# All sums of h's blocks and all lo splits on VectorE in a new order; the first gate and up pairs start with products of plain blocks

## The chip, the cores and the metric

The kernel runs on one core of a Trainium2 chip. The metric is the device time of one execution in microseconds, the median of several runs; smaller is better. The profile is of one execution, whose own time stands in the table below. Engines: TensorE (PE for matmuls, PEld for weight loads), VectorE (DVE), ScalarE (ACT), GpSimd (POOL), and SyncE (SP), whose queue issues most DMAs.

## The reference, cut to what matters

A trunk of two layers on x of 1024 tokens by 1024 channels, all float32. Layer 0 mixes tokens by sliding-window attention, layer 1 by a chunked gMLP gating unit (SGU); a conv-gated FFN follows each. The change concerns the input projections `h @ w_in` of the two FFNs and of the SGU, where h is the normalised x.

```python
def chunked_sgu(h, w_in, ln_g, ln_b, w_s, b_s, w_out):   # w_in: 1024 x 6144
    z = jax.nn.gelu(h @ w_in)
    u, v = jnp.split(z, 2, axis=-1)
    v = layer_norm(v, ln_g, ln_b)
...
    return (u * sv.reshape(B, S, SGU_HALF)) @ w_out

def conv_gated_ffn(h, w_in, conv_w, conv_b, w_out):       # w_in: 1024 x 5632
    g, u = jnp.split(h @ w_in, 2, axis=-1)
    gp = jnp.pad(g, ((0, 0), (CONV_WIDTH - 1, 0), (0, 0)))
    g = conv_b + sum(conv_w[k] * gp[:, k:k + S] for k in range(CONV_WIDTH))
    return (jax.nn.gelu(g) * u) @ w_out
...
    x = x + rms_norm(h, norm_mix_post[i])
    h = conv_gated_ffn(rms_norm(x, norm_ffn_pre[i]), ...)
    x = x + rms_norm(h, norm_ffn_post[i])
```

## The kernel before

**Split operands.** Every float32 operand of a matmul is kept as two tiles: hi, a cast to the narrower fp32r on ScalarE, and lo = operand - hi, a `tensor_tensor` subtraction. A product is three matmuls (hi·hi, hi·lo, lo·hi; `passes`). hi always comes from ScalarE. lo is made by VectorE, except that `split_eng` gives every third weight split to GpSimd; it serves `unit` (a whole weight column block, 128x1024), the `split` of `pair_unit` (128x512) and that of v's weights in `sgu` (128x1024).

**h.** `pre_norm` normalises a tile of 128 tokens; its deferred `transposes` turn it by TensorE into a PSUM bank, half a tile at a time, cast it to `hhi` and subtract to `hlo`. For the second half of tiles 0 to 3 the subtraction is done by GpSimd, which can't read PSUM, so ScalarE first copies the bank back to SBUF (L206).

**Strassen-Winograd pairs.** Two weight column blocks are multiplied with h as a 2x2 block product with seven products (`TERMS`) in place of eight: four combine sums of weight blocks S1 to S4 (`weight_sums`, made for each pair) with T1 to T3 or a plain block of h, and A22 meets T4. The sums T1 to T4 of h's blocks are made once per projection by `Blocks.steps`, in two halves q of 128x1024 each: T1 = h1a - h0a, T2 = h1b - T1, T3 = h1b - h1a, T4 = h0b - T2, with lo parts added, and each split into hi and lo (L560 the cast on ScalarE, L561 the subtraction). Before, T1 and T2 are summed on VectorE, T3 and T4 on GpSimd, and all are split on ScalarE and VectorE. `steps` is a generator that is advanced between the yields of the plain projections and then run to its end.

**The order of products.** `chain` gives it: A11·B11 into bank a, copied to p1; S2·T2 into b, u2 = b + p1; A12·B21 added on a, which is output (0,0); S1·T1 added on b, u4 = b + p1; S3·T3 into c, output (1,1) with u4; S4·B22 added on b, output (0,1); A22·T4 added on c, output (1,0) with u2. Every product of a pair is 12 matmuls of 512 columns (L683). In the SGU's v stage each block of weights uses the same seven products of 48 matmuls of 256 columns (L1138); its first block already begins with A11·B11, A12·B21 and S4·B22, on banks of their own.

**An FFN.** Columns 0 and 1 of g and u are projected plainly (`part`, `in_proj`, L140), first on the first half of the tokens, which are ready first, then on the second. Meanwhile T is made. Then ten gate pairs and ten up pairs alternate (`pair_unit`, `pair_chain`), with the convolution and the gelu between. `rawp` has two buffers, the two raw weight tiles of one pair; `wp` has eight, for the seven splits of a pair and one more. The result goes to DRAM and is read back by the out phase, which multiplies it with w_out.

**What sets the order.** The kernel runs in a TileContext that lays all instructions out before the launch: each engine has one queue, executed in order, and a planner fills these queues by a simulated timeline, in which, of the instructions that are ready, the one that stands first in the program goes first. So an engine's order can differ from the program's where something that stands later is ready sooner. Only part of the out phase fixes VectorE's order by hand. Weight loads go through SP's queue (L635 for the pairs).

## Time and profile before

| | |
|---|---|
| median of 3 runs (lowest, highest) | 2571.59 us (2565.28, 2573.16) |
| the profiled execution: time, span | 2569.5 us, 2567.8 us |
| TensorE matmuls busy | 2434.5 us, 95% of the span |
| TensorE weight loads busy | 2043.2 us, 80% |
| VectorE busy | 1848.3 us, 72% |
| ScalarE busy | 1047.4 us, 41% |
| GpSimd busy | 725.9 us, 28% |
| mean granted clock of TensorE | 0.982 of full speed |

Times in the rows are microseconds from the start of the span. Busy time is the time in which an engine executes; a share near 100% on TensorE means that matmuls follow each other without a gap, not that each is at its peak. The granted clock is a share of 2.4 GHz; 0.5 is the lower of its two levels. A duration includes the filling of the engine's pipeline, so instructions that follow each other start somewhat closer than their durations say.

### The profile page before, as it was taken

Reading aid. Unit: us, or ns where it says so; the run is one execution under the profiler, and the core shown is the slowest. Engines: PE = TensorE matmul, PEld = TensorE weight load, DVE = VectorE, ACT = ScalarE, POOL = GpSimd, SP = SyncE. Lnnn points to the kernel's source line nnn. Section 1 sums busy time; section 2 is a strip of 40 time slices with the busy share of each in tenths; the row PEclk is TensorE's granted clock in tenths of the full one; section 3 lists DMA queues with packets and bytes.
Section 4 is the critical chain, followed back from the end, with each engine's and each line's share of the span. In section 5 each row is a group of like instructions: output and inputs, shape, how many; then the busy total and the mean of one; then the engine's idle time right before and its main releaser. Section 6 shows DMA issues by size and latency. Waiting matters only on the chain.

```text
span 2567.8 us, 33884 instructions
## 1 busy us (share of the span) xinstructions
PE 2434.5 (95%) x12472; PEld 2043.2 (80%) x12472; DVE 1848.3 (72%) x2991; ACT 1047.4 (41%) x1941; POOL 725.9 (28%) x666
## 2 busy tenths in 40 slices
PE   7999988999999899979999999899997999998997
PEld 6877777888888687879997888688796888886886
DVE  5766699767666677796556765577898667666777
ACT  4655573333333444533332332444543333334443
POOL 3000035211112211361138887302254112112011
PEclk9999998999999999989999999999998999999999
DMA  7222141222226953423224445964221222249642
GB/s 221 67 49 55 50 149 49 75 90 90 67 91 212 249 151 77 156 75 116 91 90 148 141 136 184 299 203 93 90 95 48 88 90 78 80 133 286 178 98 99
DMA packets 267062, 310.50 MB, mean 121 GB/s; under 512 B 30126, under 2 KB 195344, under 8 KB 266896
## 3 DMA queue, kind: packets, MB, share of 16 engines
q1 hardware_dynamic: 249040, 275.82, 33.4%
q0 software_dynamic: 17856, 32.51, 7.5%
q8 instruction: 98, 1.61, 0.3%
q14 instruction: 68, 0.56, 0.1%
HBM read 220.72 MB, written 65.01 MB: 111 GB/s over the span
## 4 chain that ended last, share of the span: by engine, by line
PE 74%; DVE 11%; DMA 8%; issue 3%; POOL 2%; ACT 1%; SPq 1%; DVEq 0%; POOLq 0%; ACTq 0%
PE mm L683 25%; PE ob L683 10%; PE mm L772 9%; PE mm L140 6%; PE mm L1138 5%; PE ob L772 3%; PE tb L772 3%; PE ob L243 3%; DMA raw<-in_ffn_w_out 2%; PE ob L1138 2%; DVE osum L535 2%; DMA raw<-ad 2%; PE tb L1268 1%; DMA raw<-ads 1%; DVE tsum L535 1%
## 5 line engine op out<-in xcount | busy, mean ns | idle before, releaser
L683 PE MATMUL mm<-T,wsum 128*128 128x512 f32 x2496 | 601.2, 392 | 8.1 <-DVE T L535 2.9
L683 PEld LDWEIGHTS mm<-T,wsum 128*128 128x128 f32 x2496 | 467.5, 188 | 108.5 <-DVE T L535 3.9
L772 PE MATMUL mm<-osum 128*128 128x512 f32 x1644 | 400.4, 399 | 32.6 <-ACT acc L841 17.6
L772 PEld LDWEIGHTS mm<-osum 128*128 128x128 f32 x1644 | 312.5, 192 | 106.7 <-ACT acc L841 19.3
L535 DVE TENSOR_TENSOR osum<-raw,osum 128x512 fp32r<-128x512 f32 x372 | 246.1, 692 | 126.3 <-ACT osum L714 126.2
L714 ACT CAST osum<-raw 128x512 fp32r<-128x512 f32 x372 | 217.1, 619 | 284.0 <-PE tb L772 95.9
L683 PE MATMUL ob<-hhi,wsum 128*128 128x512 f32 x832 | 281.5, 397 | 22.4 <-DVE wsum L535 11.1
L642 ACT CAST wsum<-sums 128x512 fp32r<-128x512 f32 x208 | 127.5, 618 | 299.3 <-DVE sums L535 224.8
L683 PEld LDWEIGHTS ob<-hhi,wsum 128*128 128x128 f32 x832 | 158.2, 191 | 56.8 <-DVE wsum L535 11.6
L1253 POOL TENSOR_SCALAR vn<-vn,mv,rv 128x128 f32<-128x128 f32 x192 | 188.6, 994 | 45.0 <-DMA vn<-vd 21.2
L535 POOL TENSOR_TENSOR wsum<-sums,wsum 128x512 fp32r<-128x512 f32 x70 | 103.8, 1482 | 268.9 <-ACT wsum L642 227.7
L683 PE MATMUL ob<-hlo,wsum 128*128 128x512 f32 x416 | 164.6, 396 | 0.0
L535 DVE TENSOR_TENSOR wsum<-sums,wsum 128x512 fp32r<-128x512 f32 x138 | 103.4, 750 | 67.4 <-ACT wsum L642 66.6
L642 ACT CAST wsum<-raw 128x512 fp32r<-128x512 f32 x156 | 95.7, 619 | 132.7 <-PE mm L683 85.5
L772 PE MATMUL ob<-osum 128*128 128x512 f32 x480 | 131.7, 393 | 11.5 <-DVE osum L535 7.5
L683 PE MATMUL mm<-hhi,wsum 128*128 128x512 f32 x416 | 137.5, 391 | 1.6 <-DVE pu L538 1.6
L140 PE MATMUL mm<-hlo,whi 128*128 128x256 f32 (+1 forms) x416 | 136.6, 329 | 1.8 <-DVE hlo L208 1.8
L140 PE MATMUL mm<-hhi,whi 128*128 128x256 f32 (+1 forms) x416 | 136.6, 331 | 0.0
L140 PE MATMUL mm<-hhi,wlo 128*128 128x256 f32 (+1 forms) x416 | 135.9, 328 | 0.0
L997 DVE SCALAR_TENSOR_TENSOR cv<-gs,cw,cv 128x1024 f32<-128x1024 f32 (+1 forms) x96 | 124.3, 1299 | 12.4 <-ACT cv L995 11.9
L535 POOL TENSOR_TENSOR wsum<-raw,wsum 128x512 fp32r<-128x512 f32 x50 | 68.5, 1370 | 223.9 <-ACT wsum L642 179.6
L772 PE MATMUL tb<-osum 128*128 128x512 f32 x480 | 129.9, 389 | 0.0
(251 smaller groups left out, 4933.1 us busy)
## 6 DMA issues: line engine op xcount, KB each, us to landing
raw<-in_ffn_w_in SPq DMA_DIRECT2D x88, 512.0 KB, 3.9
ad<-cv SPq DMA_DIRECT2D x40, 512.0 KB, 3.8
raw<-ad SPq DMA_DIRECT2D x28, 512.0 KB, 6.4
raw<-in_ffn_w_out SPq DMA_DIRECT2D x28, 512.0 KB, 13.7
raw<-in_sgu_w_in SPq DMA_DIRECT2D x28, 512.0 KB, 4.0
xs<-xt SPq DMA_DIRECT2D x24, 512.0 KB, 3.2
vn<-vd SPq DMA_DIRECT2D x48, 256.0 KB, 3.8
ads<-ut SPq DMA_DIRECT2D x24, 512.0 KB, 5.0
```

Of the source, the lines that this page charges most:

```text
L140: nc.tensor.matmul(ps[:, cs], a[:, k, :], b[:, k, cs], start=n == 0, stop=n == 3 * KC - 1)
L243: nc.tensor.matmul(ps, a, b[:, half_of(nh)], start=n == 0 and not begun, stop=n == end, skip_group_check=begun)
L535: (eng or nc.vector).tensor_tensor(out=out, in0=a, in1=b, op=ALU.subtract)
L642: nc.scalar.copy(out=t[:, 0], in_=src)
L683: nc.tensor.matmul(bank, x, y, start=first and n == 0, stop=n == 3 * H4 - 1, skip_group_check=True)
L714: nc.scalar.copy(out=t[:, 0], in_=src)
L772: nc.tensor.matmul(self.banks[t], u, v, start=self.first and g == 0 and m == 0, stop=last and self.more is None and m == 2, skip_group_che ...
L997: nc.vector.scalar_tensor_tensor(out=cv, in0=gs[j][:, k + t0:k + t0 + n], scalar=tap_w(k, j), in1=cv, op0=ALU.mult, op1=ALU.add)
L1138: nc.tensor.matmul(bank[r][:, q * NQ:(q + 1) * NQ], x, y, start=first and q == 0 and m == 0, stop=m == 3 * H4 - 1, skip_group_check=True)
L1253: nc.gpsimd.tensor_scalar(out=vn[:, t, :], in0=vn[:, t, :], scalar1=mv[:, tt, 0:1], scalar2=rv[:, tt:tt + 1], op0=ALU.subtract, op1=ALU.mult)
L1268: nc.tensor.matmul(sv[:, t, :], vn[:, t, :], gws[(j + i) // 3][0], start=True, stop=True)
```

## The change

1. `split_eng` goes. Every weight split (`unit`, `pair_unit`, v's `split`) is done by VectorE.
2. In `transposes` the second half of tiles 0 to 3 is treated like all others: VectorE subtracts from the PSUM bank, and ScalarE's copy back to SBUF is gone.
3. `Blocks.steps` does all sums on VectorE. It makes T1 and T2 of both halves q first, splitting T2 and then T1, and only then T4 and T3 of each half. T4 is built in T2's temporary tile.
4. In an FFN the first gate pair and the first up pair use a new `first_chain` with the order A11·B11, A12·B21 (both on bank a), S4·B22 on a bank d of its own; then S2·T2 and S1·T1 on b; then S3·T3 and A22·T4 on c. `weight_sums` is called with `first`, which brings A12 and S4 forward. The gate's first five products are issued, then the up pair's weights and its first three products, then the rest of both. Later pairs are as before.
5. For the first column block of that pair the convolution, the multiplication and the output transfer are done in halves of 512 tokens, in tiles of `cvp`, which has four buffers in place of three.

```diff
--- before.py
+++ after.py
@@ -98,12 +98,6 @@
         nc.sync.dma_start(out=t, in_=row.partition_broadcast(P))
         return t
 
-    lo_turn = [0]
-
-    def split_eng():
-        lo_turn[0] += 1
-        return nc.gpsimd if lo_turn[0] % 3 == 0 else nc.vector
-
     def unit(src_aps, shape):
 
 
@@ -114,7 +108,7 @@
         hi = wp.tile(shape, F32R, name="whi", tag="w")
         lo = wp.tile(shape, F32R, name="wlo", tag="w")
         nc.scalar.copy(out=hi, in_=raw)
-        split_eng().tensor_tensor(out=lo, in0=raw, in1=hi.bitcast(F32), op=ALU.subtract)
+        nc.vector.tensor_tensor(out=lo, in0=raw, in1=hi.bitcast(F32), op=ALU.subtract)
         return hi, lo
 
     ALLS = (slice(None),)
@@ -198,14 +192,7 @@
                 for k in range(4):
                     nc.tensor.transpose(out=tp[:, k, :], in_=xn[:, tok(4 * q + k)], identity=ident)
                 nc.scalar.copy(out=hhi[:, ks], in_=tp)
-                eng = nc.vector
-                if q == 1 and t < 4:
-
-                    eng = nc.gpsimd
-                    back = xn[:, half_of(q)].rearrange("p (k q) -> p k q", q=P)
-                    nc.scalar.copy(out=back, in_=tp)
-                    tp = back
-                eng.tensor_tensor(out=hlo[:, ks], in0=tp, in1=hhi.bitcast(F32)[:, ks], op=ALU.subtract)
+                nc.vector.tensor_tensor(out=hlo[:, ks], in0=tp, in1=hhi.bitcast(F32)[:, ks], op=ALU.subtract)
 
         deferred.append(transposes)
 
@@ -563,33 +550,35 @@
             def temp():
                 return work.tile([P, 2, HALF], F32, name="tsum", tag="work")
 
-            for q in range(2):
-                ka, kb = slice(2 * q, 2 * q + 2), slice(H4 + 2 * q, H4 + 2 * q + 2)
-                t3 = temp()
-                sub_(t3, f(h1)[:, kb], f(h1)[:, ka], nc.gpsimd)
-                add_(t3, t3, f(l1)[:, kb], nc.gpsimd)
-                sub_(t3, t3, f(l1)[:, ka], nc.gpsimd)
-                yield
+            ks = [(slice(2 * q, 2 * q + 2), slice(H4 + 2 * q, H4 + 2 * q + 2)) for q in range(2)]
+            t2s = []
+            for q, (ka, kb) in enumerate(ks):
                 t1 = temp()
                 sub_(t1, f(h1)[:, ka], f(h0)[:, ka])
                 add_(t1, t1, f(l1)[:, ka])
                 yield
                 sub_(t1, t1, f(l0)[:, ka])
-                yield
                 t2 = temp()
                 sub_(t2, f(h1)[:, kb], t1)
                 yield
                 add_(t2, t2, f(l1)[:, kb])
                 split("T2", q, t2)
+                yield
                 split("T1", q, t1)
+                t2s.append(t2)
                 yield
+            for q, (ka, kb) in enumerate(ks):
+
+                sub_(t2s[q], f(h0)[:, kb], t2s[q])
+                add_(t2s[q], t2s[q], f(l0)[:, kb])
+                t3 = temp()
+                sub_(t3, f(h1)[:, kb], f(h1)[:, ka])
+                yield
+                add_(t3, t3, f(l1)[:, kb])
+                sub_(t3, t3, f(l1)[:, ka])
                 split("T3", q, t3)
                 yield
-                t4 = temp()
-                sub_(t4, f(h0)[:, kb], t2, nc.gpsimd)
-                yield
-                add_(t4, t4, f(l0)[:, kb], nc.gpsimd)
-                split("T4", q, t4)
+                split("T4", q, t2s[q])
                 yield
 
         def __getitem__(self, name):
@@ -627,7 +616,7 @@
         order = (0, 3, 1, 4, 5, 2, 6) if first else range(7)
         return [out[i] for i in order]
 
-    def pair_unit(w, c0, c1):
+    def pair_unit(w, c0, c1, first=False):
 
         raws = []
         for col in (c0, c1):
@@ -640,11 +629,11 @@
         def split(src):
             t = wp.tile([P, 2, H4, P], F32R, name="wsum", tag="w")
             nc.scalar.copy(out=t[:, 0], in_=src)
-            sub_(t[:, 1], src, t.bitcast(F32)[:, 0], split_eng())
+            sub_(t[:, 1], src, t.bitcast(F32)[:, 0])
             return t
 
         return weight_sums(raws[0][:, :H4], raws[0][:, H4:], raws[1][:, :H4], raws[1][:, H4:],
-                           sa[:, 0], sa[:, 1], sb[:, 0], sb[:, 1], split)
+                           sa[:, 0], sa[:, 1], sb[:, 0], sb[:, 1], split, first)
 
     def chain(products, p1, u2, u4, a, b, c, out):
 
@@ -672,23 +661,49 @@
         out(1, 0, c, u2)
         yield
 
+    def pair_product(wsum, name, blocks):
+        def go(bank, first):
+            n = 0
+            for k in range(H4):
+                for x, y in passes(wsum[:, 0, k, :], wsum[:, 1, k, :], *blocks[name](k)):
+                    nc.tensor.matmul(bank, x, y, start=first and n == 0, stop=n == 3 * H4 - 1,
+                                     skip_group_check=True)
+                    n += 1
+        return go
+
     def pair_chain(ws, blocks, out):
-
-
-        def product(wsum, name):
-            def go(bank, first):
-                n = 0
-                for k in range(H4):
-                    for x, y in passes(wsum[:, 0, k, :], wsum[:, 1, k, :], *blocks[name](k)):
-                        nc.tensor.matmul(bank, x, y, start=first and n == 0, stop=n == 3 * H4 - 1,
-                                         skip_group_check=True)
-                        n += 1
-            return go
 
         pu = gainp.tile([P, 2, HALF], F32, name="pu", tag="gpost")
         u2 = gainp.tile([P, 2, HALF], F32, name="u2", tag="gpre")[:, 0]
         a, b, c = out_bank(), mm_bank(), mm_bank()
-        yield from chain([product(w, t[1]) for w, t in zip(ws, TERMS)], pu[:, 0], u2, pu[:, 1], a, b, c, out)
+        yield from chain([pair_product(w, t[1], blocks) for w, t in zip(ws, TERMS)], pu[:, 0], u2, pu[:, 1], a, b, c,
+                         out)
+
+    def first_chain(ws, blocks, out, p1):
+
+        go = [pair_product(w, t[1], blocks) for w, t in zip(ws, TERMS)]
+        a, d = out_bank(), out_bank()
+        go[0](a, True)
+        nc.scalar.copy(out=p1, in_=a)
+        go[2](a, False)
+        out(0, 0, a, None)
+        go[5](d, True)
+        yield
+        u4 = gainp.tile([P, 2, HALF], F32, name="pu", tag="gpost")[:, 0]
+        u2 = gainp.tile([P, 2, HALF], F32, name="u2", tag="gpre")[:, 0]
+        b = mm_bank()
+        go[1](b, True)
+        add_(u2, b, p1)
+        go[3](b, False)
+        add_(u4, b, p1)
+        nc.scalar.copy(out=p1, in_=u4)
+        out(0, 1, d, p1)
+        yield
+        c = mm_bank()
+        go[4](c, True)
+        out(1, 1, c, u4)
+        go[6](c, False)
+        out(1, 0, c, u2)
 
 
     NPAIR = 6
@@ -998,7 +1013,7 @@
                                                in1=cv, op0=ALU.mult, op1=ALU.add)
             nc.scalar.activation(cv, cv, AF.Gelu_apprx_tanh, bias=tap_w(3, j))
 
-        with tc.tile_pool(name="gsp", bufs=2) as gsp, tc.tile_pool(name="cvp", bufs=3) as cvp:
+        with tc.tile_pool(name="gsp", bufs=2) as gsp, tc.tile_pool(name="cvp", bufs=4) as cvp:
 
             def part(j, half, parts):
                 if half == 0:
@@ -1008,7 +1023,7 @@
                 ps = in_proj(gu[j], h, half, parts)
                 yield
                 nc.scalar.copy(out=gs[j][:, 2 + half * HALF:2 + (half + 1) * HALF], in_=ps)
-                cv = cvp.tile([P, HALF], F32, name="cv")
+                cv = cvp.tile([P, HALF], F32, name="cv", tag="cv")
                 conv(j, cv, half * HALF, HALF)
                 ps = in_proj(uu[j], h, half, parts)
                 yield
@@ -1027,8 +1042,12 @@
                     run(part(j, half, 1), bs, bs, bs, bs, bs)
             run(bs)
 
-            for j in range(2 * PLAIN_FFN, nfc, 2):
+            def gate(j, first=False):
+
                 cv = {}
+
+                def cv_of(i, jj):
+                    return cv[i, jj] if first and i == 0 else cv[i][:, half_of(jj)]
 
                 def g_out(i, jj, ps, rest):
                     dst = gs[j + i][:, 2 + jj * HALF:2 + (jj + 1) * HALF]
@@ -1036,19 +1055,44 @@
                         nc.scalar.copy(out=dst, in_=ps)
                     else:
                         add_(dst, ps, rest)
-                    if i != jj:
+                    if first and i == 0:
+                        cv[i, jj] = cvp.tile([P, HALF], F32, name="cv", tag="cv")
+                        conv(j, cv[i, jj], jj * HALF, HALF)
+                    elif i != jj:
                         cv[i] = work.tile([P, S], F32, name="cv", tag="work")
                         conv(j + i, cv[i], 0, S)
 
                 def u_out(i, jj, ps, rest):
-                    dst = cv[i][:, half_of(jj)]
+                    dst = cv_of(i, jj)
                     if rest is not None:
                         add_(rest, ps, rest)
                         ps = rest
                     nc.vector.tensor_tensor(out=dst, in0=ps, in1=dst, op=ALU.mult)
-                    if i != jj:
+                    if first and i == 0:
+                        nc.sync.dma_start(out=ad[j][:, half_of(jj)], in_=dst)
+                    elif i != jj:
                         nc.sync.dma_start(out=ad[j + i], in_=cv[i])
 
+                return g_out, u_out
+
+            j0 = 2 * PLAIN_FFN
+            g_out, u_out = gate(j0, True)
+            gw = pair_unit(fw_in[layer], j0 * P, (j0 + 1) * P, True)
+            new_gs(j0)
+            new_gs(j0 + 1)
+            gc = first_chain(gw, blocks, g_out, cvp.tile([P, HALF], F32, name="p1", tag="cv"))
+            next(gc)
+            next(gc)
+            uw = pair_unit(fw_in[layer], DFF + j0 * P, DFF + (j0 + 1) * P, True)
+            uc = first_chain(uw, blocks, u_out, cvp.tile([P, HALF], F32, name="p1", tag="cv"))
+            next(uc)
+            for _ in gc:
+                pass
+            for _ in uc:
+                pass
+
+            for j in range(j0 + 2, nfc, 2):
+                g_out, u_out = gate(j)
                 gw = pair_unit(fw_in[layer], j * P, (j + 1) * P)
                 new_gs(j)
                 new_gs(j + 1)
@@ -1112,7 +1156,7 @@
                 hi = wp.tile([P, H4, NQ], F32R, name="vhi", tag="w")
                 lo = wp.tile([P, H4, NQ], F32R, name="vlo", tag="w")
                 nc.scalar.copy(out=hi, in_=src)
-                sub_(lo, src, hi.bitcast(F32), split_eng())
+                sub_(lo, src, hi.bitcast(F32))
                 return hi, lo
 
             for n in range(PLAIN_V, nb):
```

## Rows read from the trace of the kernel before

**Rows 1.** Stretches: busy us (instructions) of PE, PEld, DVE, ACT, POOL; clock; DMA.
```profile
330.00:372.00 42.00, 35.66 (x205) 26.49 (x204) 40.99 (x83) 30.06 (x75) 16.33 (x22) 1.00 0.36 127
...
400.00:460.00 60.00, 45.78 (x264) 39.76 (x264) 58.46 (x42) 21.15 (x31) 42.67 (x17) 0.89 0.12 39
460.00:805.00 345.00, 345.00 (x1524) 285.77 (x1523) 241.72 (x318) 125.66 (x188) 60.79 (x60) 1.00 0.29 91
...
1098.00:1144.00 46.00, 33.36 (x211) 30.94 (x209) 45.86 (x30) 15.32 (x19) 32.42 (x10) 0.90 0.24 79
...
1901.00:1963.00 62.00, 46.14 (x247) 38.54 (x247) 59.62 (x41) 21.00 (x31) 40.95 (x17) 0.83 0.14 42
```

**Rows 2.** Timeline, TensorE's matmuls: start, us, line, tiles, count, idle before.
```profile
419.75 0.40 PE L683 MATMUL ob<-hhi,wsum 128*128 128x512 f32 x1
...
814.78 0.50 PE L683 MATMUL mm<-hhi,wsum 128*128 128x512 f32 x1 [0.78 <-DVE pu L538]
...
820.40 0.84 PE L772 MATMUL mm<-osum 128*128 128x512 f32 x3
...
1107.23 0.40 PE L1138 MATMUL ob<-vhi,hhi 128*128 128x256 f32 x2
...
1918.83 0.40 PE L683 MATMUL ob<-hhi,wsum 128*128 128x512 f32 x1
...
2323.60 1.75 PE L772 MATMUL mm<-osum 128*128 128x512 f32 x7
```

**Rows 3.** Stretches, matmuls of L683 and of L1138 alone (count in brackets).
```profile
380.00:830.00 450.00, 385.61 (x1680) 0.98 0.30 94
...
1098.00:1180.00 82.00, 60.13 (x452) 0.92 0.28 91
```

**Rows 4.** Waits of TensorE, first FFN and SGU: us in total, times, longest.
```profile
PE ob L683 <- DVE wsum L535: 11.1, 1, 11.1
...
PE mm L1138 <- ACT T L560: 6.2, 1, 6.2
...
PE ob L1138 <- DVE vlo L535: 2.7, 1, 2.7
```

**Rows 5.** Timeline, VectorE.
```profile
399.94 2.92 DVE L535 TENSOR_TENSOR tsum<-hhi,hhi 128x1024 f32<-128x1024 f32 x1
402.90 3.32 DVE L538 TENSOR_TENSOR tsum<-tsum,hlo 128x1024 f32<-128x1024 f32 x1
...
412.44 0.68 DVE L535 TENSOR_TENSOR wsum<-sums,wsum 128x512 fp32r<-128x512 f32 x1
413.04 1.21 DVE L538 TENSOR_TENSOR tsum<-tsum,hlo 128x1024 f32<-128x1024 f32 x1
414.18 0.74 DVE L997 SCALAR_TENSOR_TENSOR cv<-gs,cw,cv 128x512 f32<-128x512 f32 x1
414.84 1.21 DVE L535 TENSOR_TENSOR T<-tsum,T 128x1024 fp32r<-128x1024 f32 x1
...
435.71 3.43 DVE L535 TENSOR_TENSOR wsum<-raw,wsum 128x512 fp32r<-128x512 f32 x2
...
458.57 0.69 DVE L538 TENSOR_TENSOR gs<-mm,pu 128x512 f32<-128x512 f32 x1
...
1155.25 1.21 DVE L535 TENSOR_TENSOR T<-tsum,T 128x1024 fp32r<-128x1024 f32 x1
```

**Rows 6.** Timeline, GpSimd.
```profile
401.86 3.27 POOL L538 TENSOR_TENSOR tsum<-tsum,hlo 128x1024 f32<-128x1024 f32 x1
```

**Rows 7.** Groups by line on GpSimd: count, busy us, mean ns, idle before.
```profile
L535 POOL TENSOR_TENSOR wsum<-sums,wsum 128x512 fp32r<-128x512 f32 x70 | 103.8, 1482 | 268.9 <-ACT wsum L642 227.7 <-DVE u L538 34.4 <-DVE cv L997 6.9
...
L535 POOL TENSOR_TENSOR wsum<-raw,wsum 128x512 fp32r<-128x512 f32 x50 | 68.5, 1370 | 223.9 <-ACT wsum L642 179.6 <-issue 44.3
...
L208 POOL TENSOR_TENSOR hlo<-xn,hhi 128x512 fp32r<-128x512 f32 x16 | 25.5, 1592 | 28.0 <-ACT xn L206 28.0
```

**Rows 8.** Timeline, SP's queue.
```profile
436.41 0.38 SPq L635 DMA_DIRECT2D raw<-in_ffn_w_in  x1
```

## The prediction

> **What bounds the kernel now.** I read the page's engine shares first, in the table above: TensorE is busy 95% of the span. What can still be gained is the few places where it stands still, and the table of stretches shows where. In a stretch of the gate pairs (460 to 805) TensorE is busy for all of 345 us, VectorE for 241.72 of it. In the three handovers (400 to 460, 1098 to 1144, 1901 to 1963) TensorE is busy for 45.78 of 60, 33.36 of 46 and 46.14 of 62 us at a mean granted clock of 0.89, 0.90 and 0.83, while VectorE is busy for practically all of each and GpSimd for two thirds [rows 1].
>
> How much is lost there follows from TensorE's timeline. A full-speed product of a pair, 12 matmuls of 512 columns, takes 2.72 us (0.2267 each; the chain of 84 comes round every 19.04 us). The first FFN's pairs begin at 419.75 and its out phase at 820.40: 400.65 us for 1680 matmuls [rows 2, 3], which need 380.9 at that pace; 19.8 are lost, 0.78 of it in a wait at the end (814.78). The second FFN, the same 1680 from 1918.83 to 2323.60, loses 23.9, its end the same. So 19.0 and 23.1 lie in the handovers. In the SGU 452 matmuls lie between 1107.23 and 1180 [rows 2, 3]; at 0.12 us each (256 columns) they need 54.2 of 72.8 us: 18.5 lost. Together 60 us, 2.3% of the span: the most that the handovers can give back.
>
> TensorE's waits name the late items: 11.1 us for a weight split on VectorE, 6.2 for the cast of a T block, 2.7 for a split in the SGU [rows 4]. The 11.1 ends with the two splits that VectorE starts at 435.71 [rows 5]: they stood in its queue behind T work. And T work is stretched. A 128x1024 tensor_tensor out of SBUF takes 2.92 and 3.32 us at 399.94 and 402.90, while GpSimd runs sums of T3 (from 401.86, 3.27 us), and 1.21 us at 413.04 and 414.84, when GpSimd does nothing [rows 5, 6].
>
> **The change, part by part.** *T blocks.* Before, VectorE runs 18 of a handover's 28 T instructions (sums of T1 and T2, all splits), GpSimd ten. From 399.94 to 459.2 VectorE executes 41 instructions: these 18, 19 of 512 columns, 4 of the convolution [rows 1, 5]. At their undisturbed spacing (1.14 from 413.04 to 414.18, 0.60 from 412.44 to 413.04, 0.66 from 414.18 to 414.84) they need 20.5 + 11.4 + 2.6 = 34.5 us; they take 59, so 24 are stretch. The change adds the ten T instructions (11.4) and the five weight splits that GpSimd did in this time (3.0): 48.9 us. VectorE is then through with all of it at 448.9, 10 us earlier than now with part of it.
>
> The price of a T instruction without GpSimd lies between 1.14 and the stretched 3.3; I take 1.14, as the rows with GpSimd idle are the same instruction on the same tiles. Here the Trainium skill (Perfetto Trace Analysis, "Optimizing Scalar/DVE Operations") speaks both ways: where VectorE is saturated, handing work to ScalarE or even GpSimd may make sense, but these two share a read port, so that moving work between them may not help. By its first half the sum would be 14.4 us more on a full VectorE in each handover; the trace, with 3.32 against 1.21, bears out the second half.
>
> *Order, and plain products first.* Within T, both halves of T2 and T1 now come before anything of T3 and T4: 14 instructions, 16 us, with the convolution and the gate's splits between them some 25, so ready at about 425. The first gate and up chains begin with three products of plain blocks each (A11·B11, A12·B21, S4·B22). From 419.75 TensorE so has six products, 16.3 us, that need no T: until 436.1. The four of T2 and T1 take it to 447.0. T3 and T4 are there at 448.9: 2 us of wait. To this I add 2.5 for products that now follow each other on one bank with an addition between (0.78 is such a wait) and for a low clock after a wait. New loss 4.5; won 14. In the second FFN VectorE starts at 1900.7 and is through at 1949.7; TensorE needs T3 at 1918.83 + 27.2 = 1946.0: loss 3.7 and 2, won 17.
>
> *SGU.* It begins with plain blocks already; the T order and the engine of the splits change. VectorE's work from 1098.4 until the last T4 split (1155.25) [rows 5], counted in the same way, is 27 instructions of 1024 columns, 5 pairs of statistics (0.67) and 2 additions: 35.4 us; with ten T instructions and two splits more, 49.1: through at 1147.5. TensorE: a first wait of 2.7 for the split of A11 as now, three plain products of 5.76 until 1127, two with T until 1138.7. T3 is there at about 1144.5, three instructions before T4: 5.8. New loss 8.5; won 10.
>
> *The other splits.* 120 weight splits go from GpSimd (1.48 and 1.37 us [rows 7]) to VectorE, 0.60 each: 72 us over 52 chains. From 460 to 805 this is 2.3 per chain, 25 us on top of 241.72 of 345 [rows 1]: 77%, hidden under TensorE's products; without that cover the 72 would count. The splits of whole weight units and of v's blocks (1.14 each) lie where VectorE has idle time.
>
> *h.* Sixteen splits of h (1.59 us on GpSimd [rows 7]) go to VectorE at 0.60, and 16 ScalarE copies vanish. Four fall into 330 to 372, where VectorE is busy 40.99 of 42 [rows 1]: no cover. Bounds per handover: nothing (GpSimd's stretch goes too), or 4 x 0.60 + 1.14 for a unit's split = 3.5. I take 1 each, 3 in all, since the last tiles of h wait for transposes as well.
>
> *Rest.* One activation tile, one output transfer more per FFN on SP, a convolution in halves (0.1 us more each): under the products.
>
> **Sum.** 14 + 17 + 10 - 3 = 38 us. The profiled execution took 2569.5 (span 2567.8); 2531.5. The median shown is 2.1 above that execution: 2534.
>
> **Rivals.** (1) *The wait moves to the up pair's weights.* Their second raw tile can be loaded only when the gate's last split is done. If VectorE again does that late, so that the load starts at 436.41 as now [rows 8], the sums follow at 442 and S4's split at 445; TensorE, through with g's five and two plain products of the up pair at 438.8, loses 8 to 10 us per FFN, and 10 in the SGU. Won 10 + 13 + 8 - 3 = 28, or 20 with one further late split: about 2547. For it: VectorE stays full until 449. Against: nothing forces this split behind T4.
> (2) *The change doesn't do what it says: the splits starve.* If all 28 T instructions go ahead of the gate's first split, the pairs begin at 431.8, 12 us late, with everything ready from then on; in the SGU 23 late. Won 6 + 10 - 4.5 - 3 = 8: 2563, the bound of what can be measured. For it: T stands first in the program. Against: now, the split at 412.44 slipped in between dependent T instructions.
> (3) *Slower: the stretch isn't GpSimd's.* VectorE's load breaks even with the 59.2 of now at (59.2 - 17.0) / 28 = 1.5 us per T instruction. At 2.2, between the two levels, it is 78.6; T4 comes at 478.5, and the pair ends 13 us later than now, three times: about 2611. In this case the rule on relieving a saturated VectorE would have been right. Against it: 1.21 at 413.04 and 414.84.
> (4) *Nearly all of the 60 comes back*, if other products fill every wait: 2514.
>
> **How the numbers follow.** Chances: forecast 0.55, (1) 0.20, (2) 0.09, (3) 0.08, (4) 0.08. A measurement of this kernel can tell about 0.3%, 8 us, from no change. Faster: 0.83 (forecast, 1 and 4); within: 0.09 (2); slower: 0.08 (3). The forecast's own range, with h at 0 to 10 and the new losses at 10 to 28: 2522 to 2546. The range, 2515 to 2557, takes in (1) and leaves out (2), (3) and part of (4).
>
> **What would show it.** In the profile after: T sums and splits near 1.21 us each in the handovers; no tensor_tensor of GpSimd but the small powers; 36 plain matmuls of the gate pair without a long wait; the first wait at T3 or T4, under 6 us; a granted clock near 1 there; the gate pairs' stretch as dense as before. The prediction is wrong if T instructions stay at 2 to 3 us, if the first product waits for a weight split, or if VectorE makes TensorE wait within the pairs.

## The result and the profile after

The changed kernel takes 2540.15 us (median, 2538.89 to 2541.5) against 2570.86 of the kernel before in the same measurement: a ratio of 0.9884 (0.9867 to 0.9901). Forecast were 2534, in a range of 2515 to 2557. The sum came out 7 us short (38 forecast, 30.7 measured), but the places in it did not come out as forecast. The profiled execution took 2541.5, its span 2539.8.

The stretches that answer to [rows 1], moved by the 7 us that the program's start is now shorter, by 4 to 9 us after that and by 17 to 19 in the second FFN, whose pairs now begin 22 us earlier (columns: busy us and instructions of PE, PEld, DVE, ACT, POOL; clock; DMA share; GB/s):

```profile
323.00:365.00 42.00, 37.68 (x213) 28.66 (x214) 38.93 (x87) 27.45 (x75) 8.56 (x18) 0.96 0.39 139
393.00:453.00 60.00, 54.64 (x305) 47.05 (x304) 56.26 (x69) 26.55 (x40) 0.30 (x3) 0.94 0.16 49
453.00:796.00 343.00, 338.87 (x1487) 278.01 (x1486) 241.80 (x352) 123.84 (x184) 3.64 (x19) 1.00 0.29 90
1092.00:1140.00 48.00, 45.85 (x343) 43.79 (x341) 45.67 (x53) 19.67 (x24) 0.00 (x0) 1.00 0.31 100
1884.00:1944.00 60.00, 54.06 (x280) 45.28 (x278) 54.07 (x68) 28.05 (x43) 0.30 (x3) 0.97 0.20 60
```

In each handover VectorE now gets far more done in the same time (69 instructions in 60 us, 42 before), GpSimd does next to nothing (at most 0.30 us), and TensorE is busier (54.64 of 60 against 45.78). VectorE's row between the handovers, 241.80 of 343, is that of before, 34 more instructions included. The 25 us that the forecast put on top for the weight splits did not come: in the kernel before, 28 of VectorE's 318 instructions in that stretch take longer than the same ones do in no_first_chain, 16.7 us in sum, while 41 splits run on GpSimd; now none does.

All 84 sums and splits of T blocks now have one duration (one tile's instructions over the whole span; the column is ns, minimum/median/maximum; after, then before):

```profile
L525 DVE TENSOR_TENSOR tsum<-tsum,hlo x24: 1205/1216/1220, 395.0 to 1924.8; 128x1024 f32<-128x1024 f32 x24
L522 DVE TENSOR_TENSOR T<-tsum,T x24: 1211/1218/1226, 406.2 to 1935.5; 128x1024 fp32r<-128x1024 f32 x24
```
```profile
L535 DVE TENSOR_TENSOR T<-tsum,T x24: 1207/1218/3422, 414.8 to 1958.2; 128x1024 fp32r<-128x1024 f32 x24
L538 DVE TENSOR_TENSOR tsum<-tsum,hlo x12: 1205/1752/3404, 402.9 to 1941.6; 128x1024 f32<-128x1024 f32 x12
```

The time by stage comes from the first matmul of each stage, as in [rows 2]; of after they are these, and of before the two that [rows 2] leaves out:

```profile
413.11 0.40 PE L669 MATMUL ob<-hhi,wsum 128*128 128x512 f32 x1
...
811.17 1.07 PE L787 MATMUL mm<-osum 128*128 128x512 f32 x4
...
1101.44 0.40 PE L1182 MATMUL ob<-vhi,hhi 128*128 128x256 f32 x2
...
1311.12 0.40 PE L669 MATMUL ob<-hhi,wsum 128*128 128x512 f32 x1
...
1585.50 0.84 PE L787 MATMUL mm<-osum 128*128 128x512 f32 x3
...
1897.18 0.40 PE L669 MATMUL ob<-hhi,wsum 128*128 128x512 f32 x1
...
2295.55 0.62 PE L787 MATMUL mm<-osum 128*128 128x512 f32 x2
```
```profile
1327.37 0.40 PE L683 MATMUL ob<-hhi,wsum 128*128 128x512 f32 x1
...
1608.16 1.07 PE L772 MATMUL mm<-osum 128*128 128x512 f32 x4
```

Their differences, and those of the experiments read in the same way (us; "FFN0" is from the first gate pair to the out phase, "out, plain v" the out phase and the SGU's plain blocks, and so on; the last stage ends with the span):

| kernel | start | FFN0 | out, plain v | SGU v | SGU u | out, plain FFN1 | FFN1 | out | span |
|---|---|---|---|---|---|---|---|---|---|
| before | 419.8 | 400.6 | 286.8 | 220.1 | 280.8 | 310.7 | 404.8 | 244.2 | 2567.8 |
| after | 413.1 | 398.1 | 290.3 | 209.7 | 274.4 | 311.7 | 398.4 | 244.2 | 2539.8 |
| no_first_chain | 411.1 | 393.2 | 291.8 | 209.2 | 274.4 | 311.1 | 392.6 | 245.9 | 2529.2 |
| T_sums_on_gpsimd | 411.1 | 408.0 | 288.6 | 215.4 | 274.4 | 310.1 | 403.3 | 245.4 | 2556.2 |
| weight_splits_on_gpsimd | 418.1 | 393.1 | 290.9 | 207.8 | 280.0 | 309.0 | 395.8 | 243.4 | 2538.1 |
| h_splits_on_gpsimd | 416.6 | 396.4 | 288.4 | 210.9 | 274.4 | 310.6 | 397.9 | 243.4 | 2538.5 |
| thirds_in_gates_only | 412.3 | 393.6 | 291.7 | 209.3 | 274.5 | 308.3 | 394.9 | 245.7 | 2530.3 |
| old_order_all_vector | 411.7 | 393.1 | 291.8 | 207.6 | 274.5 | 309.0 | 393.6 | 245.8 | 2527.1 |
| idle_gpsimd | 411.6 | 424.2 | 291.2 | 209.5 | 274.4 | 310.8 | 424.2 | 246.0 | 2591.8 |
| plain_ahead_own_banks | 411.5 | 393.0 | 290.4 | 209.7 | 274.4 | 309.1 | 394.2 | 244.3 | 2526.7 |
| sums_engine_alone | 419.8 | 393.5 | 285.3 | 212.3 | 282.9 | 310.5 | 395.7 | 244.0 | 2544.1 |
| splits_alone | 412.7 | 403.3 | 288.5 | 215.4 | 274.5 | 307.7 | 405.0 | 245.5 | 2552.6 |

The 28 us of the spans are 6.7 at the start, 2.5 in FFN0, 10.4 in SGU v, 6.4 in SGU u and 6.4 in FFN1, less 4.5 in the two plain stages. Of the 31 us forecast for the FFN handovers 9 came; 13 came from places that the forecast held at nothing or at a loss. What still stops TensorE in FFN0 (waits: us in total, times, longest):

```profile
PE mm L669 <- DVE pu L525: 4.0, 3, 2.3
...
PE mm L669 <- ACT T L547: 3.4, 1, 3.4
...
PE mm L669 <- DVE u L525: 1.7, 2, 1.5
```

The 11.1 us for a weight split of [rows 4] are gone. In their place stand a wait for T3 and the additions between two products on one bank. How the first of them comes about is in TensorE's timeline:

```profile
423.50 0.50 PE L669 MATMUL ob<-hhi,wsum 128*128 128x512 f32 x1 [0.45 <-ACT gs L1055]
...
429.14 3.06 PE L669 MATMUL mm<-T,wsum 128*128 128x512 f32 x12 [1.45 <-DVE u L525]
435.55 8.37 PE L669 MATMUL mm<-T,wsum 128*128 128x512 f32 x24 [3.36 <-ACT T L547]
443.76 0.39 PE L669 MATMUL ob<-hhi,wsum 128*128 128x512 f32 x1
```
```profile
434.45 1.04 ACT L547 CAST T<-tsum 128x1024 fp32r<-128x1024 f32 x1 [3.95 <-DVE tsum L522]
...
438.62 0.57 ACT L687 COPY p<-ob 128x512 f32<-128x512 f32 x1
```

Only four of the six plain products stand ahead of T3: those from 443.76 on are the up pair's other two. A12·B21 adds to a bank that ScalarE must first copy (438.62), and that copy stands in ScalarE's queue behind the casts of T3 and T4, which wait for VectorE's sums. S4·B22 stands there for another reason: there are two such banks, and the one that it takes over is free only when VectorE has read the gate's S4·B22 from it (437.28 to 437.96). After the wait TensorE runs its next 24 matmuls in 8.37 us, where full speed takes 5.44: its granted clock is 0.50, the lower level, from 435.55 to 441.20.

### The profile page after: what moved, and what is told of

It is laid out like the page before. It is cut to its first block, busy times and chain, and to the rows that moved or that the text cites. A ratio compares the mean times of both kernels' runs of the same rounds, so it can differ in the third digit from the quotient of the medians.

```text
span 2539.8 us, 33735 instructions
## 1 busy us (share of the span) xinstructions
PE 2429.0 (96%) x12472; PEld 2035.7 (80%) x12472; DVE 1851.3 (73%) x3184; ACT 1048.2 (41%) x1933; POOL 372.6 (15%) x477
## 4 chain that ended last, share of the span: by engine, by line
PE 81%; DVE 8%; DMA 7%; ACT 2%; issue 1%; POOL 0%; SPq 0%; DVEq 0%; POOLq 0%; ACTq 0%
PE mm L669 25%; PE ob L669 11%; PE mm L787 10%; PE mm L134 8%; PE mm L1182 5%; PE ob L230 4%; PE ob L787 3%; PE tb L787 3%; DMA raw<-in_ffn_w_out 2%; PE ob L1182 2%; PE tb L1312 2%; DMA raw<-ad 2%; DVE osum L522 2%; DMA raw<-in_sgu_w_out 1%; PE mm L230 1%; PE mm L441 1%
## 5 line engine op out<-in xcount | busy, mean ns | idle before, releaser
L669 PE MATMUL ob<-hhi,wsum 128*128 128x512 f32 x864 | 287.7, 394 | 1.2 <-ACT gs L1055 1.0
L522 DVE TENSOR_TENSOR wsum<-sums,wsum 128x512 fp32r<-128x512 f32 x208 | 142.9, 690 | 66.1 <-ACT wsum L631 66.1
L525 DVE TENSOR_TENSOR pu<-mm,pu 128x512 f32<-128x512 f32 x110 | 75.6, 688 | 99.3 <-PE mm L669 99.0
L669 PE MATMUL mm<-hhi,wsum 128*128 128x512 f32 x384 | 127.2, 392 | 3.6 <-DVE pu L525 3.6
L1012 DVE SCALAR_TENSOR_TENSOR cv<-gs,cw,cv 128x1024 f32<-128x1024 f32 (+1 forms) x100 | 115.3, 1153 | 14.7 <-issue 8.7
L1182 PE MATMUL mm<-vhi,T 128*128 128x256 f32 x640 | 119.7, 286 | 4.4 <-ACT T L547 4.3
```

Of the source, the lines that this page charges most:

```text
L522: (eng or nc.vector).tensor_tensor(out=out, in0=a, in1=b, op=ALU.subtract)
L525: (eng or nc.vector).tensor_tensor(out=out, in0=a, in1=b, op=ALU.add)
L669: nc.tensor.matmul(bank, x, y, start=first and n == 0, stop=n == 3 * H4 - 1, skip_group_check=True)
L1012: nc.vector.scalar_tensor_tensor(out=cv, in0=gs[j][:, k + t0:k + t0 + n], scalar=tap_w(k, j), in1=cv, op0=ALU.mult, op1=ALU.add)
L1182: nc.tensor.matmul(bank[r][:, q * NQ:(q + 1) * NQ], x, y, start=first and q == 0 and m == 0, stop=m == 3 * H4 - 1, skip_group_check=True)
```

## The experiments

Theory at the outset: VectorE's sums are slow only while GpSimd works beside them; off GpSimd they are quick, and six plain products cover them. Ratios are to the kernel before, with their 95% intervals.

**The plain products first.** The first gate and up pairs by the ordinary chain, as the others.

```diff
-            j0 = 2 * PLAIN_FFN
-            g_out, u_out = gate(j0, True)
...
-            for j in range(j0 + 2, nfc, 2):
+            for j in range(2 * PLAIN_FFN, nfc, 2):
```


> The changed kernel with its first gate and up pairs run by the ordinary chain again; all else as changed. The changed kernel takes about 2540. Theory (the plain products cover the T blocks): the pairs of both FFNs begin with waits again, each FFN's pair stage is some 8 to 12 us longer, 2556 to 2564; nothing moves in the SGU. Rival (VectorE without GpSimd beside it is the whole gain, and the order of the first products is worth nothing): 2538 to 2542.

2530.08 us, 0.9842 (0.9824 to 0.986). Both were wrong: without the new chain the kernel is 10 us faster than the changed one, 4.9 in FFN0 and 5.8 in FFN1. Its waits in FFN0:

```profile
PE mm L669 <- DVE pu L525: 3.4, 2, 2.6
PE mm L669 <- DVE u L525: 2.9, 2, 2.6
PE mm L669 <- DVE T L522: 0.4, 1, 0.4
```

T is in time without cover (0.4 us of wait). What is waited for is the addition between two products, which stands in VectorE's queue among the sums.

**The sums back on GpSimd.** The five kinds of sums of T3 and T4, and the old order (T3, T1, T2, T4 of one half, then of the other).

```diff
-                sub_(t3, f(h1)[:, kb], f(h1)[:, ka])
+                sub_(t3, f(h1)[:, kb], f(h1)[:, ka], nc.gpsimd)
...
```


> The changed kernel with the sums of T3 and T4 on GpSimd and in the order of before; the weight and h splits stay on VectorE and the first pairs keep their plain products. Theory (GpSimd's sums stretch VectorE's): T instructions on VectorE near 3.3 us where the two meet, 8 to 10 us lost in each of the three handovers, 2562 to 2570. Rival (the plain products cover the stretch in the FFNs): only the SGU loses its 10 us, 2548 to 2552.

2558.82, 0.9956 (0.994 to 0.9972), between the two: 9.9 us lost against after in FFN0, 4.9 in FFN1, 5.7 in SGU v. FFN0 has a wait of 7.21 us for the copy of the up pair, which here too stands in ScalarE's queue behind other work: a cast that waits for GpSimd's sum until 419.57, and an activation of the convolution that then waits 4.58 us for VectorE:

```profile
426.44 0.80 PE L667 MATMUL ob<-hhi,wsum 128*128 128x512 f32 x1 [7.21 <-ACT p L685]
```
```profile
425.20 0.72 ACT L1012 ACTIVATE cv<-cv,cw 128x512 f32<-128x512 f32 x1 [4.58 <-DVE cv L1010]
```

**The weight splits back.** Every third of them on GpSimd: of the whole units, of the pairs' sums and of v's blocks.

```diff
-        nc.vector.tensor_tensor(out=lo, in0=raw, in1=hi.bitcast(F32), op=ALU.subtract)
+        split_eng().tensor_tensor(out=lo, in0=raw, in1=hi.bitcast(F32), op=ALU.subtract)
...
```


> The changed kernel with every third weight split on GpSimd again; T and h as changed. Theory (these splits cost in three places: at the kernel's start, in the handovers, and in the SGU's second stage, where GpSimd has v's norm): the start is 4 to 5 us later, the SGU's second stage 4 to 6 us longer, the handovers 2 to 4 us each, 2555 to 2562. Rival (they lie under TensorE's products everywhere): 2538 to 2543.

2538.99, 0.9876 (0.9858 to 0.9893): no difference in sum. That is the rival's number, but not for its reason, since the splits don't lie under TensorE's products everywhere: the start loses 5.0 us and SGU u 5.6, while FFN0 wins 5.0, FFN1 2.6, SGU v 1.9 and the plain stage before FFN1 2.7.

**h's splits back.** Those of four tiles of each handover on GpSimd, from a copy, as before.

```diff
+                if q == 1 and t < 4:
+                    eng = nc.gpsimd
...
```


> The changed kernel with the splits of the second half of h's tiles 0 to 3 on GpSimd again, with ScalarE's copy. Theory (moving them cost about 1 us per handover, as the prediction has it, since VectorE is full before the handover): 2537 to 2539. Rival (the earlier start of everything after the first 100 us comes from these splits): the start is 3 to 5 us later, 2543 to 2546.

2540.3, 0.9881 (0.9862 to 0.99): no difference in sum, between the two ranges. The start loses 3.5, as the rival has it; other stages win 4.8, the two plain ones 1.9 and 1.1 of it.

**Thirds on GpSimd in the gate pairs alone.** Weight_splits_on_gpsimd had FFN0 5 us shorter than after. To see whether that can be kept without the loss elsewhere, no_first_chain, with the thirds in pair_unit's split for the gate and up pairs:

```diff
-            sub_(t[:, 1], src, t.bitcast(F32)[:, 0])
+            sub_(t[:, 1], src, t.bitcast(F32)[:, 0], nc.gpsimd if thirds and turn[0] % 3 == 0 else None)
```


> The kernel of no_first_chain (2530), with every third split of the weight sums of the gate and up pairs on GpSimd, all other splits on VectorE. Weight_splits_on_gpsimd, which had the thirds everywhere, lost 5.0 us at the start of the program and won 5.0 and 2.6 us in the two feed-forward stages. Theory: the splits on VectorE cost most at the program's start and nothing is gained by them in the gate pairs, where the two stages take 388 and 390 us instead of 393.2 and 392.6: 2521 to 2526. Rival: what the thirds won there was the queue that first_chain had built up on VectorE; with that chain gone nothing is left to win, and the total is 2528 to 2532.

2532.53, 0.9842 (0.9822 to 0.9863): the rival, 0.5 us above its range. With the first chain gone nothing is left to win.

**The engine without the order.** No_first_chain, with the loop of before in Blocks.steps (the old order), its GpSimd sums given to VectorE; against that loop:

```diff
-                sub_(t3, f(h1)[:, kb], f(h1)[:, ka], nc.gpsimd)
+                sub_(t3, f(h1)[:, kb], f(h1)[:, ka])
...
```


> The kernel of no_first_chain, with the sums of h's blocks in the order of before (T3, T1, T2, T4 of the first half, then of the second) but all on VectorE: the engine without the order. Theory: both count. T3's three instructions stand ahead of T2 in each half and the second half's T2 stands behind all ten of the first half, at 1.14 us an instruction some 3.4 and 8 us later than in no_first_chain; the product S2 T2 waits for it in all three handovers, 3 to 8 us each: 2540 to 2552. Rival: the engine is all, since the twenty sums must be through on VectorE before the first pair ends in any order: 2529 to 2534.

2528.86, 0.9826 (0.9811 to 0.9841): the rival. The new order is worth nothing that can be measured.

**GpSimd busy for nothing.** No_first_chain, with additions that nobody reads at two places of the loops in Blocks.steps, in the FFNs alone. The kernel had 32 of them at each FFN handover, twice the number that the expectation gives; its `cvp` has three buffers, beside a tile for these sums.

```diff
+                for i in range(KC):
+                    add_(self.spare, f(h1)[:, i], f(l1)[:, i], nc.gpsimd)
```


> The kernel of no_first_chain, with sixteen additions of 128x512 on GpSimd that nobody reads added at each of the two feed-forward handovers, beside the sums on VectorE; none at the gating unit's. Theory: GpSimd's work beside it is what made VectorE's sums slow. They go from 1.21 us to 2 us and more while the additions run, the first pair waits for T again, and each feed-forward stage loses 5 to 14 us: 2541 to 2558, with the gating unit's stages unchanged at 292 and 209. Rival: T_sums_on_gpsimd was slower because GpSimd's own sums came late, and the two engines don't disturb one another: VectorE's sums stay at 1.21 to 1.3 us and the time is 2529 to 2533.

2592.01, 1.0072 (1.0053 to 1.0091): slower than the kernel before. FFN0 and FFN1 take 31 us more each, every other stage what it took. The rival is out, and theory sized it too low, even if its 5 to 14 us a stage are doubled for the count. VectorE's timeline, and GpSimd's beside it:

```profile
399.56 2.31 DVE L522 TENSOR_TENSOR tsum<-hhi,hhi 128x1024 f32<-128x1024 f32 x1
401.80 2.31 DVE L525 TENSOR_TENSOR tsum<-tsum,hlo 128x1024 f32<-128x1024 f32 x1
404.03 1.78 DVE L522 TENSOR_TENSOR wsum<-raw,wsum 128x512 fp32r<-128x512 f32 x1
...
409.68 1.77 DVE L1020 SCALAR_TENSOR_TENSOR cv<-gs,cw,cv 128x512 f32<-128x512 f32 x1
...
450.70 0.68 DVE L525 TENSOR_TENSOR u<-mm,pu 128x512 f32<-128x512 f32 x1
```
```profile
391.87 26.29 POOL L525 TENSOR_TENSOR spare<-hhi,hlo 128x512 f32<-128x512 f32 x13 [9.77 <-DVE hlo L195]
...
433.10 26.05 POOL L525 TENSOR_TENSOR spare<-hhi,hlo 128x512 f32<-128x512 f32 x14
```

An instruction of 1024 columns goes from 1.22 to 2.31 us, one of 512 from 0.68 to 1.78: 1.1 us more whatever its size, and nothing more where an operand lies in PSUM (0.68 at 450.70). An instruction right behind such a one takes only 0.5 us more (0.47 at 429.98 and 451.30).

**The first chain mended.** In the changed kernel `bank` is out_bank for the gate pair and tr_bank for the up pair, and T3 and T4 are written after both pairs' plain products.

```diff
-        a, d = out_bank(), out_bank()
+        a, d = bank(), bank()
         go[0](a, True)
         nc.scalar.copy(out=p1, in_=a)
+        go[5](d, True)
         go[2](a, False)
         out(0, 0, a, None)
-        go[5](d, True)
...
```


> The changed kernel with its first_chain mended: the up pair's plain products go to two other banks, S4 B22 stands between A11 and A12 so that the copy of the partial sum has time, and the sums T3 and T4 are written after the plain products of both pairs, so that ScalarE's copy for the up pair stands before their casts. Theory: the chain cost 10 us because the up pair's last two plain products were held up by that copy and by a bank, and so did not stand before the wait for T3; mended, all of them cover the sums, and the time is 2522 to 2531. Rival: it costs because the up pair's splits and the 512-column steps stand ahead of the sums on VectorE, and because plain products are cover that VectorE at full speed doesn't need; the time stays at 2536 to 2542.

2532.13, 0.9838 (0.982 to 0.9856): 8 of the 10 us are back, 1 us above theory's range. All six plain products now stand ahead of T3, and the first wait over a microsecond comes at 444.22:

```profile
444.22 3.94 PE L669 MATMUL mm<-T,wsum 128*128 128x512 f32 x10 [2.13 <-DVE wsum L522]
```

But it is no faster than the kernel with no first chain at all (0.9842).

**Each half of the change alone.** First the kernel before, with the GpSimd sums on VectorE and nothing else:

```diff
-                sub_(t3, f(h1)[:, kb], f(h1)[:, ka], nc.gpsimd)
+                sub_(t3, f(h1)[:, kb], f(h1)[:, ka])
...
```


> The kernel before, with the five kinds of GpSimd additions in the sums T3 and T4 given to VectorE, in their old order, and nothing else changed. Theory: this edit wins what was won at the three handovers, and the weight splits that stay on GpSimd keep the program's start (418 to 420) and the gating unit's second half (280) as they were: feed-forward stages 393 to 396, 2536 to 2544. Rival: the whole of it is this edit, 2526 to 2533. A second rival: without the other splits VectorE still runs beside GpSimd's splits at the handovers and the sums stay slow, 2550 to 2560.

2546.15, 0.9899 (0.9884 to 0.9914): 26.4 us won, the time 2 us above theory's range: FFN0 7.1, SGU v 7.8, FFN1 9.1 by the stages.

Then the other half, no_first_chain with the loop of before in Blocks.steps:

```diff
-                sub_(t3, f(h1)[:, kb], f(h1)[:, ka])
+                sub_(t3, f(h1)[:, kb], f(h1)[:, ka], nc.gpsimd)
...
```


> The kernel before, with all weight splits and all of h's splits on VectorE, but the sums T3 and T4 on GpSimd in their old order and the ordinary chain for the first pair (T_sums_on_gpsimd without the first chain). Theory: the feed-forward stages go back to before's 401 to 405 and the gating unit's to 288 and 215, while the start and the gating unit's second half keep what the splits win: 2548 to 2556; first_chain cost T_sums_on_gpsimd some 7 us by a copy that stood behind late sums. Rival: first_chain covered late sums after all, and without it the time is 2560 to 2570, as before.

2554.42, 0.9931 (0.9915 to 0.9948): 18.1 us won, as theory has it, 7.1 of it at the start, 6.3 in SGU u. T_sums_on_gpsimd, which differs by the first chain alone, is at 0.9956: that chain may cost with late sums too, about 4 us by the two medians and not 7; but the intervals overlap, and of the two FFNs only FFN0 is longer with it (408.0 against 403.3).

The two halves add up: 26.4 and 18.1 are 44.5, and old_order_all_vector, which is both (but for `cvp`'s fourth buffer, which splits_alone has too), wins 44.2 (2573.04 less 2528.86). The rest of the change, order and first chain, gives back some 11 to 14 of it (2540.15 less 2528.86; 44.2 less 30.7); the first chain's part is the 10 us of no_first_chain.

## Why the prediction was right, and where it was not

**VectorE's price, right.** 1.14 us a T instruction was taken because GpSimd's sums were held to be what stretches it. The 84 instructions of after are all at 1.20 to 1.23 us, and idle_gpsimd brings the stretch back with work that nobody reads. The sum over VectorE's rows in FFN0's handover (395 to 462) of what each kind takes beyond its duration in no_first_chain is about 31 us there, and the stage loses 31.0, as if nothing hid any of it. Rival 3 is out; what it would have cost idle_gpsimd shows, with T instructions at 2.2 us: FFN0 24 us and FFN1 19 longer than before, where 13 each were worked out, since the 512-column steps are stretched as well. By the Trainium skill (Perfetto Trace Analysis, "Optimizing Scalar/DVE Operations") a full VectorE may be relieved by GpSimd, but may not be helped by it for the read port that VectorE and GpSimd share; the runs bear out the second half, with 26.4 us for taking five kinds of sums off GpSimd.

**VectorE's end, too early by 12 us.** It was to be through at 448.9, 48.9 us after the first sum of T at 399.94. In the changed kernel that sum starts 6.7 us earlier, so the same work would end at 442.1. The last T split ends at 453.9 (452.72, 1.22 us), 60.7 us after the first sum:

```profile
393.24 1.22 DVE L522 TENSOR_TENSOR tsum<-hhi,hhi 128x1024 f32<-128x1024 f32 x1
...
449.17 0.69 DVE L1070 TENSOR_TENSOR cv<-ob,cv 128x512 f32<-128x512 f32 x1 [2.73 <-PE ob L669]
...
452.72 1.22 DVE L522 TENSOR_TENSOR T<-tsum,T 128x1024 fp32r<-128x1024 f32 x1
```

The price of one instruction was right, the number was not: VectorE ran 69 instructions in that time where the forecast counted 56 (41 and 15), since splits and sums of the up pair and of the next gate pair, and more of the convolution, went ahead of T4, and it stood still for 2.7 us until TensorE had a product ready. In FFN1 it is 59.4 us against 49.

**Six products as cover: the step that failed.** The forecast had TensorE need T3 at 447, 27 us behind the first pair's start, and lose 4.5 us with 14 won in FFN0, and 17 in FFN1. It needed T3 at 432.2 (429.14 and 3.06), 19 us behind that start, with four plain and two T products done, and FFN0 takes 17.2 us more than the 380.9 of its matmuls. Won were 2.5 and 6.4. Nor was the cover needed: without the chain 7.4 and 12.2 are won, T3 and T4 in time. Mended, all six products stand ahead of T3, and that wins nothing over the ordinary chain. The chain was read as products alone; its copies and additions, and the queues that they stand in, were priced at 2.5 us in all.

**The FFN handovers were oversized even so.** With sums at full speed and no first chain 12 us remain in each (393.2 and 392.6 less 380.9), not 4.5 and 5.7: in FFN0 waits of 6.7 us, for the additions u and pu that stand among VectorE's sums, and a low clock behind them. After the first of these waits 12 matmuls take 4.50 us, where full speed takes 2.72 (granted clock 0.62 from 424.77 to 429.00, and 0.50 in its first 2 us):

```profile
424.77 4.50 PE L669 MATMUL mm<-T,wsum 128*128 128x512 f32 x12 [2.60 <-DVE u L525]
```

**SGU, right.** Won 10.4 where 10 was forecast; its waits are 4.3 for a cast of T and 1.0 for a split of A11, forecast 5.8 and 2.7.

**The other splits and h: wrong in sign.** Forecast were nothing for the weights and a loss of 3 for h. In splits_alone they win 18 us together. Where that lies TensorE's waits show, at the start (0 to 120 us) and in SGU u, for before, after and weight_splits_on_gpsimd:

```profile
PE mm L334 <- DVE hlo L208: 5.1, 3, 3.6
...
PE tb L1268 <- POOL vn L1253: 4.4, 5, 1.6
```
```profile
PE mm L321 <- DVE hlo L195: 1.1, 3, 0.4
...
PE tb L1312 <- POOL vn L1297: 0.3, 1, 0.3
```
```profile
PE tb L1318 <- POOL vn L1303: 3.1, 5, 1.2
```

At the start it is h's splits on VectorE that come late, and VectorE itself waits 3.6 us there for GpSimd's splits of h; in SGU u it is v, which GpSimd normalises, and that wait comes back with the weight splits. Both are GpSimd's splits in the way of something else, VectorE's work in one case and GpSimd's own in the other, and the forecast looked for cover on VectorE alone. These waits explain 4 us of the 6.7 and 4 of the 6.4; the rest is open. The 1 us for h in each handover may have been right: h_splits_on_gpsimd wins 1.9 and 1.1 us in the two plain stages. That either kind alone can go back to GpSimd without loss in sum (0.9876 and 0.9881 against 0.9884) is shown only for the kernel with the first chain. There, it seems, a shorter VectorE queue in the first pair wins back what is lost elsewhere: thirds_in_gates_only wins nothing once the chain is gone, and without the chain both kinds together lose 17 us (sums_engine_alone against old_order_all_vector). Neither kind was put back alone in a kernel without the chain. Why the plain stages win a few us in those two runs is open.

**Rivals.** (1) did not come: the sums of the up pair's weights started at 419.65 (forecast for that case: 442). (2) did not come: the first product of the pair began without a wait. (3) is out, as said above. (4) was not reached by any kernel; the fastest, old_order_all_vector, stands at 0.9826 (2528.86 against 2514).

So the forecast's nearness to the median is in part luck, two errors that partly cancel: 22 us too many for the FFNs (31 for 9), and 13 us from the start and SGU u that it did not have. The plain stages lost 4.5, where it had 3 for h.

## What to carry to other kernels

Where VectorE is full, a step handed to GpSimd isn't free of VectorE: here a 512-column step on GpSimd held up about one VectorE instruction by 1.1 us, and doing the step on VectorE takes 0.6. Before putting products ahead as cover, list what else they need besides operands, here a bank, a copy and an addition, and what stands in front of those in the queues. Change the engine first and alone: here it gave all of the 44 us, while the new order gave nothing that could be measured and the new chain took 10.

## What the runs showed of the hardware

The stretch is a fixed hold per GpSimd instruction, not a slower rate. In idle_gpsimd nearly every VectorE instruction with two SBUF operands takes 1.1 us more while GpSimd works, of 512 columns or of 1024; in [rows 5, 6] GpSimd's instructions have 1024 columns and VectorE's sum takes 2.1 us more (3.32 against 1.21). In sums_engine_alone these two of GpSimd's occasional splits hold up one instruction each:

```profile
409.01 3.72 POOL L535 TENSOR_TENSOR wsum<-raw,wsum 128x512 fp32r<-128x512 f32 x1 [20.72 <-ACT wsum L642]
...
415.77 1.52 POOL L535 TENSOR_TENSOR wsum<-sums,wsum 128x512 fp32r<-128x512 f32 x1 [2.34 <-ACT wsum L642]
```
```profile
409.76 1.22 DVE L535 TENSOR_TENSOR tsum<-hhi,tsum 128x1024 f32<-128x1024 f32 x1
410.89 0.68 DVE L535 TENSOR_TENSOR wsum<-sums,wsum 128x512 fp32r<-128x512 f32 x1
411.50 1.78 DVE L997 SCALAR_TENSOR_TENSOR cv<-gs,cw,cv 128x512 f32<-128x512 f32 x1
...
416.06 1.78 DVE L535 TENSOR_TENSOR wsum<-sums,wsum 128x512 fp32r<-128x512 f32 x1
```

The split at 409.01 lasts 3.72 us while VectorE's instructions run at their own 0.68 and 1.2, until one of them takes 1.04 us longer. That is how the Trainium skill describes the two engines' shared port pair (SBUF — State Buffer, "SBUF: two separate sides"): one of them holds it for a whole instruction and the other is blocked. The trace agrees on the block: 1.1 us for a hold by a 512-column instruction, 2.1 by one of 1024, whatever VectorE runs. The hold is somewhat shorter than the GpSimd instruction by its row (1.30 us for a split of 512 columns that meets no VectorE instruction with two SBUF operands, at 458.03 in sums_engine_alone). Why two VectorE instructions went ahead while the split at 409.01 waited, no run shows.
